# A transformer layer on one core: a second place for the turned attention output, a tile of its own for its squares, and the last group's squares from PSUM

## The chip, the core and the metric

The kernel runs on one core of one Trainium2 chip. Its engines run at the same time, each through its own queue of instructions: TensorE (PE, with its weight loads as PEld), VectorE (DVE), ScalarE (ACT), GpSimd (POOL) and SyncE (SP), which here only issues DMAs. SBUF is the on-chip memory of 128 partitions, PSUM the matmuls' accumulator memory. The metric is the device time of one execution in microseconds. Before the change it is 2869.16 us, the median of three runs (2869.08 to 2871.89).

## The reference

One layer is computed for two streams that share weights: 256 prompt tokens and 2048 latent tokens of 1024 channels. All data is float32.

```python
q, k, v, f = project(rms_norm(x, norm1_g) * (1 + sc1) + sh1, w_in, q_g, k_g)   # 4 heads, 2 halves of 64
# one head, 128 queries; latent queries see 512 cached + 2048 latent keys
s = einsum('bqhmd,bkhmd->bhmqk', q, k) / 8
p = softmax(s)                                   # for m = 0 and m = 1
a = p[:, :, 0] - lam * p[:, :, 1]
o = einsum('bhqk,bkhe->bqhe', a, v)
# the other half of the channels: real part of a 2-D DFT over positions and 128 channels
four = fft2(f, axes=(positions, channels), norm='ortho').real @ w_four
mix = concat([rms_norm(o, subln_g) * (1 - lam_init), four]) @ w_out
x = x + g1 * mix
x = x + g2 * square(relu((rms_norm(x, norm2_g) * (1 + sc2) + sh2) @ w1)) @ w2
```

The change lies in `rms_norm(o)`: for each query and head it needs the sum of the squares of the 128 outputs. Outputs are the new x of both streams and the prompt's keys and values.

## The kernel before, in words

**Stages.** The program runs the input projection (to about 470 us of the span), the DFT with its linear map (to about 517), attention (517 to about 1257), the output projection, and the MLP to the end. Float32 products are built from three matmuls of split operands (lines 94 to 97: high by high, low by high, high by low), so each operand is split beforehand into a rounded part and a rest: `ah` and `al` in attention, `woh` and `wol` for w_out, `mh` and `ml` for the mixed tokens.

**The DFT's end.** Its result stands in four tiles `ys0` to `ys3` (line 747), one for each channel group, 8192 bytes a partition each. When a tile is complete, GpSimd issues its store to the DRAM tensor `four` (line 830). These stores go through the software DMA queues, whose completion counters are called DMASW0 to DMASW7.

**Attention.** There are four heads of eight groups of 256 latent tokens, and one prompt group in each head. A latent group has two query tiles j, each with two halves m, so four stages, each with five score tiles of 128 x 512 (2560 keys). A stage runs so: PE fills five PSUM banks `Ss` (line 1081), VectorE takes the maximum of each (line 1086) and of the five (line 1089), ScalarE writes the five exponentials (line 1105) into a tile `P0` (m = 0; 10240 bytes) or two tiles `P1` (m = 1) and adds them up in `sms`. GpSimd combines P0 and P1 to the attention weights (lines 1120 and 1121). PE transposes these (line 1136), ScalarE and VectorE split the transposes into `ahs` and `als` (lines 1143 and 1148), and PE multiplies them with the values into the left half of a PSUM bank `po`.

**The end of a group**, around which the change is made: `o1` copies the output, which stands channel by token, to SBUF on ScalarE (`oTs`, line 1173). `o2` turns it on PE into the right half of the same bank (line 1177). `o3` copies the turned output to SBUF on VectorE (tile `o`, line 1181), `o4` squares its two halves on ScalarE with a sum over each row into `oss` (line 1187), and GpSimd goes on from there (`o5` to `o9`: the inverse root, a pass through DRAM that spreads it over partitions, the product with oT, and the store to the DRAM tensor `att`).

**What sets the order.** In attention every piece of work is an event with a time that is written in the code, `add(t, fn)`, in units of a stage T of 5.2. The events are sorted by that time and emitted, so the order on each engine is that of the table. For the last group (head 3, group 7, `self.last`) `o3` stands close behind `o2`, and `o4` to `o9` are kept in a list `LASTO` and called in the output projection, where the w_out splits (`w_split`, line 1560), the split of the mixed tokens (`mix`, line 1588) and the matmuls (`out_mm`, line 1599) are written one after another:

```python
mix(s0); w_split(1, 1, 4); out_mm(s0, 1, 0, 2)
for fn in LASTO[:2]: fn()          # o4, o5
w_split(1, 4); out_mm(s0, 1, 2, 4)
for fn in LASTO[2:]: fn()          # o6 to o9
```

**Where tiles lie.** Pools take SBUF one behind the other. The pool `at` (line 995) holds o, oss and the other small tiles of attention; the pool `ap` (line 996), which lies right behind it, holds the five places of P0. The DFT's pools have been given back by then, so attention's tiles lie on bytes that the DFT used, and the first user of such bytes waits until their last user is done. In the built program ys3 lies on bytes 75776 to 83967 of each partition. The first place of P0 begins at byte 83072, 896 bytes before the end of ys3.

Of the kernel before, what the change touches and what calls it, by code (L numbers as in the profile page):

```python
# [11 lines left out]
F32 = mybir.dt.float32  # L12
F32R = mybir.dt.float32r
AF = mybir.ActivationFunctionType
# [5 lines left out]
P = 128  # L20
# [21 lines left out]
def body(tc, a, out):  # L42
    nc = tc.nc
    ctx = ExitStack()
    with ctx:
# [944 lines left out]
        with ExitStack() as c3_:  # L990
# [49 lines left out]
            class Group:  # L1040
# [136 lines left out]
                        nc.tensor.transpose(self.po[:, 256 + j * P:256 + j * P + P], self.oT[:, j * P:j * P + P], ident)  # L1177

                def o3(self):
                    self.o = self.op.tile([P, 256], F32, tag="o", name=f"o{self.nm}", bufs=1)  # L1180
                    nc.vector.tensor_copy(self.o, self.po[:, 256:512])

                def o4(self):
                    self.oss = self.op.tile([P, 4], F32, tag="oss", name=f"oss{self.nm}")
                    for j in range(2):
                        o = self.o[:, j * P:j * P + P]
                        nc.scalar.activation(o, o, AF.Square, accum_out=self.oss[:, j:j + 1])

                def o5(self):
                    nc.gpsimd.tensor_add(self.oss[:, 0:2], self.oss[:, 0:2], self.s0e)  # L1190
# [115 lines left out]
            for h in range(H):  # L1306
# [19 lines left out]
                for g in range(hd.ng):  # L1326
                    gr = Group(hd, g)
                    add(base - (4 if h or g > 1 else 3) * T + 0.6 * u if base else -3.03 * T, gr.qload)
                    for st in range(4):
                        j, m = divmod(st, 2)  # L1330
# [640 lines left out]
        with ExitStack() as c6:  # L1971
# [62 lines left out]
            with tc.manual_schedule():  # L2034
                pend, NM, loaded, KS = None, 7 * 24, 4, []
                for i in range(7):
                    for b in range(3):
                        ps = [pp.tile([P, 512], F32, tag="ps", name=f"ps{i}_{b}_{j}", bufs=6) for j in range(3)]
                        for k in range(16):
# [19 lines left out]
                            if (i, b) == (6, 2) and 9 <= k < 12:  # L2059

                                j = k - 9
# [86 lines left out]
```

## Time and profile before

| | us |
|---|---|
| median of three runs | 2869.16 (2869.08 to 2871.89) |
| the profiled execution's own time | 2869.73 |
| its span in the trace | 2867.9 |
| PE busy | 2824.6 (98%) |
| VectorE busy | 1989.6 (69%) |
| ScalarE busy | 1533.1 (53%) |
| GpSimd busy | 1075.7 (38%) |
| mean granted clock of PE | 0.995 |

The profile is one execution. A row of its groups gives line, engine, operation, output and input, the count, the busy time, the mean of one in ns, and then the idle time of that engine just before these instructions with what ended most of it. A timeline row gives the start in us from the span's start, the length, the engine and the instruction, and in brackets the idle time before it with its releaser; "x4" is a run of four alike. The granted clock is a share of PE's full speed.

### The profile page before, as it was taken

To read this page: it belongs to the slowest core of one execution; us is meant where nothing else is said; L and a number is where in the kernel's file an instruction comes from. 1 tells how busy PE (TensorE), PEld (TensorE's weight loads), DVE (VectorE), ACT (ScalarE), POOL (GpSimd) and SP (SyncE) were. 2 spreads that over 40 slices of the span, in tenths; PEclk is the share of its full clock that TensorE was granted. 3 is DMA by queue.
4 is the path that set the end of the run, shared out by engine and by line. 5 is a ranking of instruction groups with operands and counts; after the bars stand their busy time and mean duration, and the time that the engine had idled before them with its cause. 6 is when DMAs were issued, how large, how long until landed. Compare 5 with 4: busy or idle time off the path is not lost.

```text
span 2867.9 us, 43210 instructions
## 1 busy us (share of the span) xinstructions
PE 2824.6 (98%) x15029; PEld 2455.1 (86%) x15029; DVE 1989.6 (69%) x3357; ACT 1533.1 (53%) x3479; POOL 1075.7 (38%) x890
## 2 busy tenths in 40 slices
PE   8999999799999999999999999999999999999999
PEld 5888888588888888888889999999998888888887
DVE  7767786688888888864477777778775354345554
ACT  4333332698998989853356565556554332233221
POOL 1211223589999899942223333333332000000000
PEclk9999999899999999999999999999999999999999
DMA  7777767331332322247777676667657464445663
GB/s 284 220 207 205 233 202 251 148 107 38 83 86 54 111 44 66 79 110 212 242 223 233 221 249 228 216 224 236 231 175 250 145 203 138 140 143 182 206 207 110
DMA packets 404492, 497.70 MB, mean 174 GB/s; under 512 B 31427, under 2 KB 320304, under 8 KB 401202
## 3 DMA queue, kind: packets, MB, share of 16 engines
q1 hardware_dynamic: 398656, 484.09, 53.5%
q0 software_dynamic: 2064, 7.67, 0.8%
q10 hardware_dynamic: 3554, 3.17, 0.3%
q8 instruction: 119, 1.95, 0.3%
q14 instruction: 99, 0.81, 0.1%
HBM read 317.30 MB, written 179.62 MB: 173 GB/s over the span
## 4 chain that ended last, share of the span: by engine, by line
PE 53%; DVE 1%; DMA 0%; issue 0%; ACT 0%; SPq 0%; POOL 0%; DVEq 0%
PE ps L95 8%; PE ps L96 8%; PE ps L97 8%; PE pB L1765 2%; PE pB L1763 2%; PE pB L1764 2%; PE pA L1763 2%; PE pC L1763 2%; PE pC L1765 2%; PE pA L1764 2%; PE pC L1764 2%; PE pA L1765 2%; PE po L97 2%; PE po L96 2%; PE po L95 2%; PE pD L1765 1%
## 5 line engine op out<-in xcount | busy, mean ns | idle before, releaser
L1086 DVE TENSOR_REDUCE mxs<-Ss 128x1 f32<-128x512 f32 x636 | 405.6, 686 | 95.3 <-PE Ss L1081 85.0
L1440 DVE TENSOR_TENSOR sl<-sr,sh 128x768 fp32r<-128x768 f32 x168 | 161.8, 964 | 331.5 <-ACT sh L1439 331.1
L1121 POOL TENSOR_TENSOR P0s<-P0s,P1s 128x1024 f32<-128x1024 f32 (+2 forms) x128 | 378.7, 2959 | 10.7
L1439 ACT CAST sh<-sr 128x768 fp32r<-128x768 f32 x168 | 140.6, 838 | 418.2 <-PE ps L96 418.2
L1805 POOL TENSOR_TENSOR gs<-g,g 128x384 f32<-128x384 f32 x48 | 69.7, 1452 | 469.4 <-ACT g L1775 389.5
L1105 ACT ACTIVATE P1s<-Ss,mxs 128x512 f32<-128x512 f32 x318 | 215.1, 693 | 40.2 <-DVE mxs L1089 38.4
L95 PE MATMUL pj<-wh,hh 128*128 128x512 f32 x576 | 228.9, 397 | 2.0 <-DVE hh L556 2.0
L95 PE MATMUL ps<-thT,sh 128*128 128x512 f32 x585 | 227.6, 389 | 0.0
L96 PE MATMUL ps<-tlT,sh 128*128 128x512 f32 x585 | 227.6, 389 | 0.0
L97 PE MATMUL ps<-thT,sl 128*128 128x512 f32 x585 | 227.6, 389 | 0.0
L96 PE MATMUL pj<-wl,hh 128*128 128x512 f32 x576 | 227.0, 394 | 0.0
L97 PE MATMUL pj<-wh,hl 128*128 128x512 f32 x576 | 225.8, 392 | 0.0
L1105 ACT ACTIVATE P0s<-Ss,mxs 128x512 f32<-128x512 f32 x318 | 214.3, 691 | 17.3 <-DMA four<-ys 16.7
L1081 PE MATMUL Ss<-KS1s,Qs 128*128 128x512 f32 x636 | 188.3, 420 | 14.8 <-ACT P0s L1105 14.5
L1136 PE MATMUL pts<-ident,P0s 128*128 128x128 f32 x1280 | 191.8, 273 | 4.8 <-DVE als L1148 1.8
L1081 PE MATMUL Ss<-KS0s,Qs 128*128 128x512 f32 x636 | 190.2, 420 | 0.4 <-ACT P1s L1105 0.4
L1774 ACT ACTIVATE g<-uz 128x384 f32<-128x384 f32 x144 | 75.8, 526 | 200.1 <-DVE uz L1797 173.7
L1136 PEld LDWEIGHTS pts<-ident,P0s 128*128 128x128 f32 x1280 | 151.4, 140 | 36.2 <-issue 4.5
L1120 POOL TENSOR_SCALAR P1s<-P1s,tots 128x1024 f32<-128x1024 f32 (+2 forms) x128 | 171.3, 1338 | 5.8
L1148 DVE TENSOR_TENSOR als<-pts,ahs 128x512 fp32r<-128x512 f32 x256 | 163.7, 681 | 8.7 <-ACT ahs L1143 8.6
L95 PE MATMUL ps<-ophT,sh 128*128 128x512 f32 x423 | 164.7, 389 | 1.1 <-DVE uz L1797 1.1
L96 PE MATMUL ps<-oplT,sh 128*128 128x512 f32 x423 | 164.6, 389 | 0.0
(535 smaller groups left out, 8020.4 us busy)
## 6 DMA issues: line engine op xcount, KB each, us to landing
sr<-sd SPq DMA_DIRECT2D x84, 768.0 KB, 4.5
a<-in_w SPq DMA_DIRECT2D x184, 256.0 KB, 4.1
sd<-gs SPq DMA_DIRECT2D x192, 192.0 KB, 1.9
sd<-g SPq DMA_DIRECT2D x144, 192.0 KB, 2.1
wm<-in_w_mod SPq DMA_DIRECT2D x32, 512.0 KB, 5.2
Qs<-qd SPq DMA_DIRECT2D x32, 512.0 KB, 5.4
b<-in_w SPq DMA_DIRECT2D x64, 256.0 KB, 5.4
b<-tsum SPq DMA_DIRECT2D x64, 256.0 KB, 4.7
```

The costliest lines, as they stand in the source:

```text
L95: nc.tensor.matmul(ps, lh, rh, start=first, stop=False)
L96: nc.tensor.matmul(ps, lh, rl, start=False, stop=False)
L97: nc.tensor.matmul(ps, ll, rh, start=False, stop=last)
L1081: nc.tensor.matmul(S[:, :w], self.Q[:, x, m, j * P:j * P + P], self.hd.KS[m][:, b * 512:b * 512 + w], start=(x == 0), stop=(x == 1))
L1086: nc.vector.tensor_reduce(self.mx[j][:, m, b:b + 1], self.S[j, m, b], axis=AX.X, op=ALU.max)
L1105: nc.scalar.activation(dst, S, AF.Exp, bias=self.mx[j][:, m, 6:7], accum_out=self.sm[j][:, m, b:b + 1])
L1120: nc.gpsimd.tensor_scalar(p, p, tot[:, 3:4], 0.0, op0=ALU.mult, op1=ALU.add)
L1121: nc.gpsimd.tensor_add(d, d, p)
L1136: nc.tensor.transpose(pt[:, c:c + P], self.p0[j][:, (kb + t) * P:(kb + t + 1) * P], ident)
L1763: nc.tensor.matmul(ps, wh[:, c], hh[:, k, :], start=first and k == 0, stop=False, skip_group_check=True)
L1764: nc.tensor.matmul(ps, wh[:, c], hl[:, k, :], start=False, stop=False, skip_group_check=True)
L1765: nc.tensor.matmul(ps, wl[:, c], hh[:, k, :], start=False, stop=k == 3, skip_group_check=True)
```

## The change

`o3` copies into one of two places for o, where there was one. For the last group it copies nothing: `o4` then reads the turned output from the PSUM bank. `o4` writes the squares, which nothing reads, into a tile `osq` of its own with one place, where before they were written over o. From there on the line numbers of the changed kernel are 3 higher.

```diff
 def o3(self):
-    self.o = self.op.tile([P, 256], F32, tag="o", name=f"o{self.nm}", bufs=1)
+    if self.last:
+        self.o = self.po[:, 256:512]
+        return
+    self.o = self.op.tile([P, 256], F32, tag="o", name=f"o{self.nm}", bufs=2)
     nc.vector.tensor_copy(self.o, self.po[:, 256:512])

 def o4(self):
     self.oss = self.op.tile([P, 4], F32, tag="oss", name=f"oss{self.nm}")
+    osq = self.op.tile([P, P], F32, tag="osq", name=f"osq{self.nm}", bufs=1)
     for j in range(2):
-        o = self.o[:, j * P:j * P + P]
-        nc.scalar.activation(o, o, AF.Square, accum_out=self.oss[:, j:j + 1])
+        nc.scalar.activation(osq, self.o[:, j * P:j * P + P], AF.Square, accum_out=self.oss[:, j:j + 1])
```

The pool `at` grows by 1024 + 512 bytes a partition, so P0's first place begins at byte 84608 in the changed program, 640 bytes behind the end of ys3.

The rows below are instructions in the order in which an engine runs them, with output, input and shape. A name ends in the tile's number in its own build, which differs between the two. Behind "waits" stand the counters that the instruction waits for before it starts: PE_49, DVE_49, Activation_49 and Pool_49 are those of the engines (an engine that waits for its own counter waits for its own earlier work), DMASW and DMAHW those of software and hardware DMA queues.

ScalarE, where the DFT ends and attention begins; L760 and L811 are copies of the DFT's last pieces. Before:

```order
L811 COPY abl_1_5204<-pabl_1_5201 128x130 [waits PE_49,Activation_49]
L760 COPY yu<-py 128x129 [waits PE_49] x2
L1105 ACTIVATE P0s_0_0_5289,sms_0_0_5266<-Ss_0_0_0_0_5268,mxs_0_0_5265 128x512 [waits DMASW0_49,DVE_49,Pool_49]
...
L1105 ACTIVATE P1s_0_0_0_5323,sms_0_0_5266<-Ss_0_0_1_0_5292,mxs_0_0_5265 128x512 [waits DVE_49,Activation_49]
...
L1105 ACTIVATE P0s_0_1_5357,sms_0_1_5330<-Ss_0_1_0_0_5332,mxs_0_1_5329 128x512 [waits DMASW7_49,DMASW3_49,DVE_49]
```

Now:

```order
L811 COPY abl_1_5204<-pabl_1_5201 128x130 [waits PE_49,Activation_49]
L760 COPY yu<-py 128x129 [waits PE_49] x2
L1105 ACTIVATE P0s_0_0_5289,sms_0_0_5266<-Ss_0_0_0_0_5268,mxs_0_0_5265 128x512 [waits DVE_49,Pool_49]
...
L1105 ACTIVATE P1s_0_0_0_5323,sms_0_0_5266<-Ss_0_0_1_0_5292,mxs_0_0_5265 128x512 [waits DVE_49,Activation_49]
...
L1105 ACTIVATE P0s_0_1_5357,sms_0_1_5330<-Ss_0_1_0_0_5332,mxs_0_1_5329 128x512 [waits DMASW4_49,DMASW3_49,DMASW7_49,DMASW0_49,DVE_49]
```

The first exponential has lost its wait on DMASW0, which stood at the count 80, that of the store of ys3. The second P0 tile now lists four such counters, DMASW0 at 64 and the others at 48. The stores' own DMAs were issued behind waits for these same counts. The second P1 tile of that place waits for DMASW5 at 64, the store of ys0, before and now.

ScalarE, at the end of one of the 31 other groups (head 0, group 1), with the copy that VectorE makes for it in the first row. Before:

```order
L1181 COPY os_1_6209<-po 128x256 [waits PE_49]
L1143 CAST ahs_2_12_6258<-pts_2_12_6242 128x512 [waits PE_49,Activation_49]
L1187 ACTIVATE os_1_6209,osss_1_6275<-os_1_6209 128x128 [waits DVE_49]
L1187 ACTIVATE os_1_6209,osss_1_6275<-os_1_6209 128x128
L1105 ACTIVATE P1s_4_0_0_6281,sms_4_0_6138<-Ss_4_0_1_0_6220,mxs_4_0_6137 128x512 [waits DVE_49,Pool_49]
...
L1143 COPY ahs_2_14_6322<-pts_2_14_6288 128x512 [waits PE_49,Activation_49]
```

Now:

```order
L1184 COPY os_1_6210<-po 128x256 [waits PE_49]
L1143 CAST ahs_2_12_6259<-pts_2_12_6243 128x512 [waits PE_49,Activation_49]
L1190 ACTIVATE osqs_1_6277,osss_1_6276<-os_1_6210 128x128 [waits DVE_49]
L1190 ACTIVATE osqs_1_6277,osss_1_6276<-os_1_6210 128x128 [waits Activation_49]
L1105 ACTIVATE P1s_4_0_0_6283,sms_4_0_6139<-Ss_4_0_1_0_6221,mxs_4_0_6138 128x512 [waits DVE_49,Pool_49]
...
L1143 COPY ahs_2_14_6324<-pts_2_14_6290 128x512 [waits PE_49]
```

The order is the old one. The second square now waits for ScalarE's own first one, and splits of transposes that come after the squares have lost such a wait.

VectorE, where attention ends and the output projection begins. Before:

```order
L1148 TENSOR_TENSOR als_7_18_14838<-pts_7_18_14816,ahs_7_18_14834 128x512 [waits DVE_49,Activation_49]
L1181 COPY os_7_14860<-po 128x256 [waits PE_49,Activation_49]
L1566 SCALAR_TENSOR_TENSOR wol_0_14923<-wout_13409,cols,woh_0_14915 128x512 [waits DMAHW6_49,Pool_49]
L1592 CAST mh_14944<-wout_13411 128x1024 [waits DMAHW2_49,DMAHW3_49,DMASW4_49,DMAHW6_49,DMASW3_49,DMAHW7_49,DMASW2_49,DMASW1_49]
L1593 TENSOR_TENSOR ml_14945<-wout_13411,mh_14944 128x1024 [waits DMAHW3_49,DVE_49]
```

Now:

```order
L1148 TENSOR_TENSOR als_7_18_14869<-pts_7_18_14847,ahs_7_18_14865 128x512 [waits DVE_49,Activation_49]
L1569 SCALAR_TENSOR_TENSOR wol_0_14952<-wout_13434,cols,woh_0_14944 128x512 [waits DMAHW6_49,Activation_49,Pool_49]
L1595 CAST mh_14973<-wout_13436 128x1024 [waits DMAHW2_49,DMAHW3_49,DMASW4_49,DMAHW6_49,DMASW3_49,DMAHW7_49,DMASW2_49,DMASW1_49]
L1596 TENSOR_TENSOR ml_14974<-wout_13436,mh_14973 128x1024 [waits DMAHW3_49,DVE_49]
L1569 SCALAR_TENSOR_TENSOR wol_1_14953<-wout_13434,cols,woh_1_14945 128x512 [waits Activation_49]
```

The copy that waited for PE's transposes is gone from VectorE's queue, and the splits behind it stand directly after the last `als`; wol_0 itself now names ScalarE, whose woh_0 it reads. On ScalarE the first of the last group's squares, in its old place behind woh_0 to woh_3 and the copy `oTs`, waits for PE where it waited for VectorE. On GpSimd the last group's sum `o5` stands one place earlier, ahead of the issue of an `att` store.

## The prediction

> **What bounds the kernel now.** I read the page first: shares by engine, then the groups with idle time before them.
>
> ```profile
> span 2867.9 us, 43210 instructions
> PE 2824.6 (98%) x15029; PEld 2455.1 (86%) x15029; DVE 1989.6 (69%) x3357; ACT 1533.1 (53%) x3479; POOL 1075.7 (38%) x890
> ...
> L1105 ACT ACTIVATE P0s<-Ss,mxs 128x512 f32<-128x512 f32 x318 | 214.3, 691 | 17.3 <-DMA four<-ys 16.7
> L1081 PE MATMUL Ss<-KS1s,Qs 128*128 128x512 f32 x636 | 188.3, 420 | 14.8 <-ACT P0s L1105 14.5
> ```
>
> PE is busy for 98%, so only a microsecond in which PE stands still or runs slowly can be won. One such hole stands out: PE waited 14.5 us for exponentials, and these had waited 16.7 us for a DMA that has nothing to do with attention, the store of the Fourier result. The timeline places it, PE, ScalarE, VectorE and GpSimd in turn:
>
> ```profile
> 520.34 0.61 PE L1081 MATMUL po<-KS1s,Qs 128*128 128x512 f32 x2
> 534.71 2.08 PE L1081 MATMUL Ss<-KS1s,Qs 128*128 128x512 f32 x4 [13.75 <-ACT P0s L1105]
> ```
>
> ```profile
> 533.88 0.69 ACT L1105 ACTIVATE P0s<-Ss,mxs 128x512 f32<-128x512 f32 x1 [16.69 <-DMA four<-ys]
> ...
> 537.80 0.69 ACT L1105 ACTIVATE P1s<-Ss,mxs 128x512 f32<-128x512 f32 x1 [0.47 <-DVE mxs L1089]
> ...
> 541.75 0.69 ACT L1105 ACTIVATE P0s<-Ss,mxs 128x512 f32<-128x512 f32 x1 [0.50 <-DVE mxs L1089]
> ...
> 545.19 0.69 ACT L1105 ACTIVATE P1s<-po,mxs 128x512 f32<-128x512 f32 x1
> ...
> 548.51 0.71 ACT L1105 ACTIVATE P0s<-Ss,mxs 128x512 f32<-128x512 f32 x1
> ```
>
> ```profile
> 520.98 0.16 DVE L1089 TENSOR_REDUCE mxs<-mxs 128x1 f32<-128x5 f32 x1
> ```
>
> ```profile
> 515.03 0.56 POOL L830 DMA_DIRECT2D four<-ys  x1 [5.56 <-DVE ys L769]
> ...
> 518.57 0.53 POOL L830 DMA_DIRECT2D four<-ys  x1 [0.34 <-issue]
> ```
>
> The landing of the first and of the last of the four stores (views of these two alone):
>
> ```profile
> DMA to landing us min/median/max: 9.7/9.7/9.7
> ```
>
> ```profile
> DMA to landing us min/median/max: 15.2/15.2/15.2
> ```
>
> The last store lands at 518.57 + 15.2 = 533.8, and the first exponential starts at 533.88. Its row maximum was there at 521.14. Then the clock, in windows (time, length, busy PE, PEld, DVE, ACT, POOL, clock, DMA):
>
> ```profile
> 523.00:524.00 1.00, 0.00 (x0) 0.00 (x0) 0.00 (x0) 0.00 (x0) 0.00 (x0) 0.53 1.01 419
> ...
> 534.00:538.00 4.00, 3.29 (x8) 2.57 (x9) 1.83 (x4) 3.53 (x11) 0.00 (x0) 0.50 0.00 1
> 540.00:545.00 5.00, 4.50 (x17) 2.53 (x15) 4.73 (x12) 4.50 (x14) 2.54 (x4) 0.99 0.03 3
> 550.00:560.00 10.00, 7.95 (x31) 4.28 (x30) 8.20 (x17) 9.66 (x28) 9.65 (x7) 1.00 0.00 1
> 600.00:1240.00 640.00, 637.00 (x4119) 541.71 (x4119) 551.76 (x1089) 574.09 (x1614) 592.70 (x473) 1.00 0.30 75
> ```
>
> Half clock until about 540, then full. From 600 to 1240 PE idles 3 us in 640 while ScalarE has 66 us free. The second hole is at attention's end, PE and then VectorE and ScalarE:
>
> ```profile
> 1254.19 0.28 PE L97 MATMUL po<-ahs,Vs 128*128 128x256 f32 x1
> 1254.94 0.44 PE L1177 MATMUL po<-ident,oTs 128*128 128x128 f32 x2 [0.46 <-ACT oTs L1173]
> 1257.32 0.77 PE L95 MATMUL po<-woh,mh 128*128 128x512 f32 x1 [1.94 <-DVE mh L1592]
> ...
> 1263.77 0.40 PE L97 MATMUL po<-woh,ml 128*128 128x512 f32 x1
> ...
> 1266.09 0.39 PE L95 MATMUL po<-woh,mh 128*128 128x512 f32 x1
> ```
>
> ```profile
> 1251.09 1.29 DVE L1148 TENSOR_TENSOR als<-pts,ahs 128x512 fp32r<-128x512 f32 x2 [2.37 <-ACT ahs L1143]
> 1255.48 0.42 DVE L1181 COPY os<-po 128x256 f32<-128x256 f32 x1 [3.10 <-PE po L1177]
> 1255.82 0.74 DVE L1566 SCALAR_TENSOR_TENSOR wol<-wout,cols,woh 128x512 fp32r<-128x512 f32 x1
> 1256.48 0.69 DVE L1592 CAST mh<-wout 128x1024 fp32r<-128x1024 f32 x1
> ...
> 1262.74 0.69 DVE L1592 CAST mh<-mT 128x1024 fp32r<-128x1024 f32 x1
> 1263.53 1.23 DVE L1593 TENSOR_TENSOR ml<-mT,mh 128x1024 fp32r<-128x1024 f32 x1
> ```
>
> ```profile
> 1251.42 2.58 ACT L1565 ACTIVATE woh<-wout,cols 128x512 fp32r<-128x512 f32 x4
> ```
>
> VectorE stood 3.10 us before the copy of the last group's turned output, with the output projection's first operands queued behind it; PE stood 1.94 us for one of these, and its clock was halved again:
>
> ```profile
> 1256.00:1257.00 1.00, 0.00 (x0) 0.00 (x0) 1.00 (x2) 1.00 (x5) 0.00 (x0) 0.96 1.01 287
> 1257.00:1263.00 6.00, 5.68 (x13) 4.01 (x14) 5.97 (x10) 6.00 (x12) 0.55 (x1) 0.50 0.94 259
> ```
>
> **The change, part by part.** *Two places for o.* The copy waits for PE alone at nearly every group (order rows above), so a second place removes no wait: 0 by itself.
>
> *What the added bytes do.* o's second place and the squares' own tile add 1024 + 512 bytes in the pool ahead of P0, so P0 slides 1536 bytes, off ys3. The order rows show it: the first exponential no longer waits on DMASW0. It then waits for its row maximum: 521.14, say 521.2. Gain 533.88 - 521.2 = 12.7 us. What is late next? The second P0 tile now lists four DMA counters, but at counts that the four stores' own issues had already waited for, so these passed by 518.57. The P1 tile that lies on ys0 needs ys0's store: 515.03 + 9.7 = 524.7, while its exponential, the third of the stage at 545.19, comes near 534 in the new time. Neither holds. On SyncE three loads of the prompt's keys and values list other counters, at counts of transfers that were over before; their order is the old one, as is that of every store.
>
> On top of it comes the clock. Four stages of five exponentials took 548.51 - 533.88 = 14.63, where the tightest took 3.32 (545.19 to 548.51), so four take 13.28 when nothing is late. The slips, 1.35 in all, begin where PE ran at 0.50. Now PE would stand only from 520.95 (520.34 + 0.61) to the first exponential's end near 521.9; the clock stayed up through idle pieces of the window 550 to 560. I take 1.0 of the 1.35 (bounds 0 and 1.35). Head: 13.7 (12.7 to 14.0).
>
> *The last group's copy leaves VectorE.* Its queue goes on after als, at 1251.09 + 1.29 = 1252.4; woh_0 is done near 1252.1. So wol_0, mh and ml, which took from 1255.82 to 1258.4, are through near 1255, when the transposes end at 1255.38. PE loses the 1.94. With idle of only 0.46 the clock should not drop: 24 steps from the first to the 25th projection matmul took 1266.09 - 1257.32 = 8.77; at the pace of the last ten, (1266.09 - 1263.77) / 10 = 0.232, they take 5.57. The 25th would start at 1255.38 + 5.57 = 1260.95, 5.1 sooner. Then VectorE is next: the second tile's mh came 1262.74 - 1255.82 = 6.9 after wol_0, so 1259.3, and up to 0.7 later because wol_4 to wol_7 still wait for ScalarE, which squares first; ml is done 2.0 later, 1261.3 to 1262.0, and PE wants it at 1261.4. I take 0.4 off: 4.7. Bounds: 1.9 (only the pause goes) and 5.1. The last group's squares, now from PSUM, start after the transposes instead of after the copy, so ScalarE comes to woh_4 a little sooner; the last group's normalisation behind them feeds token tiles that come much later, 0. On GpSimd one add of that group stands a place further ahead, also 0.
>
> A rule speaks against the larger value. The Trainium skill, TensorE: Matmul & The Clock Gate, Part 1 (The HAM clock gate), puts the fall to half clock after an idle window of about 3.4 us. By it the pieces here, 0.46 and 1.94 with work between, would not have caused the dip, and only the 1.94 would come back. The trace is quicker than that: at the head PE stopped at 520.95 and the clock was 0.53 in 523 to 524, under 3.1 us later, and here it was 0.96 over 1256 to 1257 and 0.50 after, so it fell near 1256.96, 2.5 us after the last full row of matmuls ended (1254.19 + 0.28). I follow the rows, and the other case is a rival below.
>
> *Squares into their own tile.* The second square now waits for the first, since both write one tile, 31 times and once at the end. Rows of a pair, and of a pair where the second must wait:
>
> ```profile
> 592.91 0.24 ACT L1187 ACTIVATION_READ_ACCUMULATOR os<-os 128x1 f32 x1
> 593.00 0.34 ACT L1187 ACTIVATE os<-os 128x128 f32<-128x128 f32 x1
> ...
> 593.85 0.69 ACT L1105 ACTIVATE P1s<-Ss,mxs 128x512 f32<-128x512 f32 x1 [0.42 <-DVE mxs L1089]
> ```
>
> ```profile
> 1701.05 0.53 ACT L1774 ACTIVATE g<-uz 128x384 f32<-128x384 f32 x1 [2.38 <-DVE uz L1797]
> 1701.60 0.53 ACT L1775 ACTIVATE g<-g 128x384 f32<-128x384 f32 x1
> ```
>
> In the first view the second square starts before the first one's sum is read out; in the other the second works on what the first wrote. The overlap of 0.15 (592.91 + 0.24 - 593.00) goes: 0.15 a group, 4.7 in all on ScalarE. Queued behind are the next stage's exponentials, for whose banks PE waits. Here the pair is followed by an idle 0.42, which hides it, and ScalarE has 66 us free; three or four waits for its own old work vanish too. I take 0 on PE; without that cover 4.7 lost.
>
> **Sum.** 13.7 + 4.7 = 18.4. The profiled execution took 2869.73 (span 2867.9 and 1.8 around it), 0.57 over the median of 2869.16. 2869.73 - 18.4 = 2851.3, from the median 2850.8: I say 2851.
>
> **Rivals.** *Dip stays:* the clock falls at attention's end all the same, since the short transposes and the 0.46 before them stay; 13.7 + 1.9 = 15.6, 2854. For it: between 1254.47 and 1255.38 PE still works for half the time only; against it: the clock stayed at 1.00 through 550 to 560, where PE was busy for 7.95 of 10. (The Trainium skill's rule above would end at this time too.) *Squares show:* 18.4 - 4.7 = 13.7, 2855.5. For it: ScalarE is 90% busy; against it: the idle that follows. *The wait moves:* the second P0 tile holds until the stores land, so that its stage, at 541.75 before, starts at 533.88: 7.9 + 4.7 = 12.6, 2857; were nothing freed, 4.7, 2865. For it: it lists DMASW0; against it: the counts. *Slower:* the wait between the squares costs so much that ScalarE becomes attention's bound. The 66 us that ScalarE has free are 66 / 31 = 2.1 a group; beyond these each further microsecond is PE's, and from 18.4 / 31 = 0.6 more, so from 2.7 a group, the gain is eaten up. At 3 us a group the time would be 2869.7 - 18.4 + 31 x 0.9 = 2879. For it: the wait stands 31 times in the stage that is fullest; against it: the pair at 1701, where the waiting square starts 0.02 after the first one's end (1701.05 + 0.53 to 1701.60).
>
> **How the numbers follow.** Forecast 0.68, dip stays 0.14, squares show 0.08, wait moves 0.06 (half of it at 2857), slower 0.02, other 0.02. The forecast's own range is 2849 to 2853; the rivals to 2857 belong in, and 2848 allows for more slips saved in the ramp. A measurement here tells 0.2%, 5.7 us. All cases but the slower and a remainder pass it, though 2865 does not: faster 0.95, same 0.03, slower 0.02.
>
> **What would show it.** No idle of 16 us before the first P0 exponential; it starts near 521 and PE's gap there is about 1 us at clock 1.00. The second P0 stage has no DMA as releaser. PE's 1.94 before mh is gone, and the window after it reads 1.00. Between the squares stands about 0.15. A P0 group still released by a store, or PE idle between 600 and 1240 well above 3 us, would make me wrong.

## The result, and where the time went

The changed kernel takes 2861.71 us (median of 8 runs, 2856.99 to 2863.5). The kernel before, run beside it, takes 2870.54 us (8 runs, 2867.7 to 2873.44). The ratio is 0.9967, with a 95% interval of 0.9956 to 0.9978. It is 0.3% faster, by about half of what was forecast, and outside the range of 2848 to 2857. The profiled execution took 2860.23, with a span of 2858.4 after 2867.9.

The start of attention did what was forecast. The page's groups, and the timelines of ScalarE and PE in the changed kernel:

```profile
L1105 ACT ACTIVATE P0s<-Ss,mxs 128x512 f32<-128x512 f32 x318 | 214.3, 691 | 4.9 <-DVE mxs L1089 4.0
L1081 PE MATMUL Ss<-KS1s,Qs 128*128 128x512 f32 x636 | 187.7, 420 | 1.7 <-ACT P0s L1105 1.4
```

```profile
521.25 0.69 ACT L1105 ACTIVATE P0s<-Ss,mxs 128x512 f32<-128x512 f32 x1 [4.02 <-DVE mxs L1089]
```

```profile
517.08 2.54 PE L1081 MATMUL Ss<-KS0s,Qs 128*128 128x512 f32 x10
...
522.08 1.40 PE L1081 MATMUL Ss<-KS1s,Qs 128*128 128x512 f32 x4 [1.10 <-ACT P0s L1105]
```

The DMA is gone as a releaser, the exponential starts 12.6 us sooner, and PE waits 1.10 us for it instead of 13.75.

The end of attention did it too, at first. PE there:

```profile
1240.98 0.44 PE L1177 MATMUL po<-ident,oTs 128*128 128x128 f32 x2 [0.46 <-ACT oTs L1173]
1241.17 0.48 PE L95 MATMUL po<-woh,mh 128*128 128x512 f32 x1
...
1246.86 0.39 PE L95 MATMUL po<-woh,mh 128*128 128x512 f32 x1
...
1247.84 0.50 PE L97 MATMUL po<-woh,ml 128*128 128x512 f32 x1 [0.36 <-DVE ml L1596]
```

The projection starts right behind the transposes and runs at full pace. The 25th matmul (1246.86) comes 19.2 us sooner than before. Then something happens that the prediction does not mention:

```profile
1263.62 0.39 PE L97 MATMUL po<-woh,ml 128*128 128x512 f32 x1
1271.62 1.97 PE L249 MATMUL ptb<-ident,xn 128*128 128x128 f32 x8 [7.62 <-DVE xn L236]
```

These are the transposes of the first output tile after its RMSNorm. Before the change PE stood 1.06 us at this place:

```profile
1283.63 1.09 PE L249 MATMUL ptb<-ident,xn 128*128 128x128 f32 x8 [1.06 <-DVE xn L236]
```

VectorE's scaled tile `xn` is late because GpSimd's inverse root `nrsb` (line 92) is late. GpSimd's timeline of the changed kernel shows what stands ahead of it:

```profile
1239.60 0.64 POOL L1193 TENSOR_TENSOR osss<-osss,s0es 128x2 f32<-128x2 f32 x1
1240.32 1.68 POOL L92 TENSOR_TENSOR osss<-osss,mhalf 128x2 f32<-128x2 f32 x1
1242.30 0.66 POOL L1201 DMA_DIRECT2D rs<-osss  x1 [0.29 <-POOL osss L92]
1250.33 0.55 POOL L1206 DMA_DIRECT2D rbs<-rs  x1 [7.38 <-DMA rs<-osss]
1256.56 0.73 POOL L1211 TENSOR_TENSOR oTs<-oTs,rbs 128x256 f32<-128x256 f32 x1 [5.67 <-DMA rbs<-rs]
...
1259.40 0.59 POOL L1201 DMA_DIRECT2D rs<-osss  x1 [0.29 <-POOL osss L92]
1262.77 0.54 POOL L1206 DMA_DIRECT2D rbs<-rs  x1 [2.78 <-DMA rs<-osss]
1268.57 0.72 POOL L1211 TENSOR_TENSOR oTs<-oTs,rbs 128x256 f32<-128x256 f32 x1 [5.26 <-DMA rbs<-rs]
1269.59 0.58 POOL L1215 DMA_DIRECT2D att<-oTs  x1 [0.30 <-POOL oTs L1211]
1270.20 0.58 POOL L92 TENSOR_TENSOR nrsb<-nssb,mhalf 128x1 f32<-128x1 f32 x1
```

and, on VectorE, what the root waits for:

```profile
1262.95 0.15 DVE L230 TENSOR_SCALAR nssb<-nssb 128x1 f32<-128x1 f32 x1 [1.22 <-ACT nsqb L229]
1270.81 0.75 DVE L236 TENSOR_SCALAR xn<-xo,nrsb 128x1024 f32<-128x1024 f32 x1 [7.71 <-POOL nrsb L92]
```

The mean square was there at 1263.10. The root came at 1270.20, because the last two groups' roots go through DRAM one after the other, and GpSimd waits with its whole queue for the store and then for the load, before the product and its store, twice. Before the change the same chain read:

```profile
1252.79 0.20 POOL L1190 TENSOR_TENSOR osss<-osss,s0es 128x2 f32<-128x2 f32 x1
1253.07 0.69 POOL L92 TENSOR_TENSOR osss<-osss,mhalf 128x2 f32<-128x2 f32 x1
1254.06 0.66 POOL L1198 DMA_DIRECT2D rs<-osss  x1 [0.29 <-POOL osss L92]
1259.45 0.55 POOL L1203 DMA_DIRECT2D rbs<-rs  x1 [4.73 <-DMA rs<-osss]
...
1277.79 0.58 POOL L1212 DMA_DIRECT2D att<-oTs  x1 [0.30 <-POOL oTs L1208]
1282.21 0.58 POOL L92 TENSOR_TENSOR nrsb<-nssb,mhalf 128x1 f32<-128x1 f32 x1 [3.84 <-DVE nssb L230]
```

There GpSimd was through at 1278.37 and stood 3.84 us for the mean square. Counted from the last transposes (1254.94 and 1240.98), PE's side now wants the root 5.0 us sooner (1282.11 - 1254.94 = 27.17, now 1263.10 - 1240.98 = 22.12). GpSimd is free for it 5.8 us later (1278.37 - 1254.94 = 23.43, now 1270.17 - 1240.98 = 29.19). 5.0 + 5.8 less the slack of 3.7 (1282.11 - 1278.37) makes the 7.1 us for which the root is late.

The pause also halves the clock. Windows of the changed kernel (time, length, busy PE, PEld, DVE, ACT, POOL, clock, DMA):

```profile
1240.00:1254.00 14.00, 13.18 (x60) 10.29 (x59) 13.80 (x21) 7.71 (x17) 3.13 (x4) 1.00 0.89 240
...
1271.60:1274.00 2.40, 2.38 (x10) 2.28 (x11) 1.26 (x2) 1.02 (x2) 0.00 (x0) 0.50 0.55 195
1274.00:1276.00 2.00, 2.00 (x7) 1.52 (x6) 1.18 (x3) 2.00 (x8) 0.55 (x1) 0.50 0.91 284
...
1277.00:1278.00 1.00, 1.00 (x6) 0.81 (x5) 0.59 (x1) 0.00 (x0) 0.00 (x0) 1.00 0.80 240
```

So the dip at attention's end is gone (1.00 over 1240 to 1254), and one of the same kind stands 30 us later.

The span falls into three parts by three rows of PE's timeline: attention's first matmul, the last transposes, and the first output tile's transposes. For the profiled executions:

| us | attention | transposes to first output tile | from there to the end |
|---|---|---|---|
| before | 737.90 | 28.69 | 1584.27 |
| changed | 723.90 | 30.64 | 1586.78 |
| difference | -14.00 | +1.95 | +2.51 |
| forecast | -13.7 | -4.7 | 0 |

The sum of the differences is -9.54, and attention starts 0.04 later: the 9.5 between the spans.

### The profile page after: what moved, and what is told of

Its sections match the earlier page's. It is cut to its first block, busy times and chain, and to the rows that moved or that the text cites. A ratio compares the mean times of both kernels' runs of the same rounds, so it can differ in the third digit from the quotient of the medians.

```text
span 2858.4 us, 43061 instructions
## 1 busy us (share of the span) xinstructions
PE 2822.7 (99%) x15029; PEld 2452.7 (86%) x15029; DVE 1988.8 (70%) x3356; ACT 1536.9 (54%) x3479; POOL 1077.5 (38%) x890
## 3 DMA queue, kind: packets, MB, share of 16 engines
q8 instruction: 119, 1.95, 0.3%
## 4 chain that ended last, share of the span: by engine, by line
PE 91%; DMA 4%; DVE 2%; ACT 1%; issue 1%; POOL 1%; SPq 0%; ACTq 0%; DVEq 0%; POOLq 0%
PE Ss L1081 10%; PE ps L95 8%; PE ps L97 8%; PE ps L96 8%; PE pts L1136 5%; PE po L95 4%; PE po L96 4%; PE pj L97 4%; PE po L97 4%; PE pj L96 4%; PE pj L95 4%; PE pB L1768 2%; PE pB L1767 2%; PE pB L1766 2%; PE pA L1767 2%; PE pA L1768 2%
```

## The experiments

The theory: the late root on GpSimd costs the 6.7 + 2.5 us that the last two columns lack. The rivals: the chain is late whenever attention ends early; the loads or the clock hold PE there for a reason of their own; the squares' wait for each other costs the time in attention. In the tables below the same three parts are given for each run's profile (attention starts between 516.6 and 519.3 us in them, by the stages ahead of it, so the parts compare better than the spans), and the ratio is that of its runs to runs of the kernel before on the same chip.

### Each part of the change alone

The address alone, in the kernel before:

```diff
+shift(c3_.enter_context(tc.tile_pool(name="a_pad", bufs=1)), 1024, "p")   # 1024 unused bytes
 ap = c3_.enter_context(tc.tile_pool(name="a_p", bufs=5, reuse_waits="tile"))
```

> The kernel before with 1024 unused bytes ahead of the P0 pool and nothing else: P0's first place begins at byte 84096, behind ys3. Theory (GpSimd's queue: in the changed kernel the first output tile's normalisation waits on GpSimd behind the last group's pass through DRAM, and the 7.62 us for which PE then stands, with the half clock after it, give back 9 of the 18.4): here attention and the GpSimd work behind it move together, so the first exponential starts near 521.2, PE's idle before the first output tile's transposes stays near 1.1, and the whole gain of 14.0 reaches the end: span about 2854, faster than the changed kernel. Rival (an earlier end of attention by itself makes GpSimd or the loads late): PE stands several us before those transposes here too, and the gain is 9 or less.

The last group's squares alone, in the kernel before:

```diff
 def o3(self):
     self.o = self.op.tile([P, 256], F32, tag="o", name=f"o{self.nm}", bufs=1)
+    if self.last:
+        return
     nc.vector.tensor_copy(self.o, self.po[:, 256:512])
 ...
-        nc.scalar.activation(o, o, AF.Square, accum_out=self.oss[:, j:j + 1])
+        src = self.po[:, 256 + j * P:256 + j * P + P] if self.last else o
+        nc.scalar.activation(o, src, AF.Square, accum_out=self.oss[:, j:j + 1])
```

> The kernel before with the last group's squares read from PSUM (written to o as before, one place, no own tile), P0 where it was. Theory (GpSimd's queue): the projection starts 4.6 to 5.3 us earlier in relation to attention's end, but GpSimd's chain does not come earlier, so PE stands 2 to 7.6 us before the first output tile's transposes, where it stood 1.06; the time is between 0 and 4.5 us longer than before (4.5 is what is left if the changed kernel's 9.5 is the padding's 14.0 and this part). Rival (the missing 9 us lie in attention, in the squares' wait for each other): this part alone gives its 4.7 us, span about 2863.

The changed kernel with one place for o, so that P0 lies 384 bytes inside ys3 again:

```diff
-    self.o = self.op.tile([P, 256], F32, tag="o", name=f"o{self.nm}", bufs=2)
+    self.o = self.op.tile([P, 256], F32, tag="o", name=f"o{self.nm}", bufs=1)
```

> The changed kernel with one place for o: P0's first place begins at byte 83584, 384 bytes inside ys3. Theory (the gain at attention's start is the address alone): the first exponential waits for the last store again and starts near 533.9, and the time is that of the run with the PSUM squares alone, within 1 us, since the squares' wait for each other costs PE nothing. Rival (the second place for o, or the squares' own tile, gives the gain): it starts near 521 and the time stays near the changed kernel's. Rival (the squares' wait costs): up to 4.7 us longer than the run with the PSUM squares alone.

And the changed kernel again:

> The changed kernel once more, to stand beside the other runs on the same chip. Theory: PE's idle before the first output tile's transposes is again about 7.6 us and the small store's round trip about 8 us, since both follow from the order and the loads: the time is 9 us under the kernel before. Rival (that profile caught a late DMA by chance): the idle is 1 to 3 us and the time 16 us under it.

| | median us (runs) | ratio, 95% | attention | to first output tile | to the end |
|---|---|---|---|---|---|
| address alone | 2859.07 (5) | 0.9959, 0.9946 to 0.9973 | 724.62 | 28.64 | 1584.31 |
| PSUM squares alone | 2876.09 (11) | 1.0017, 1.0009 to 1.0026 | 737.67 | 31.39 | 1586.80 |
| one place for o | 2876.20 (11) | 1.0017, 1.0008 to 1.0026 | 737.69 | 30.56 | 1585.82 |
| changed, again | 2862.75 (5) | 0.9967, 0.9955 to 0.9980 | 725.42 | 30.63 | 1585.83 |

1024 bytes that nothing reads bring at least as much as the whole change: 12.6 us by the medians and 13.3 by the parts, where 14.0 were expected. By the parts it is more than the change, which loses time in the last two; by the runs that is not clear. These five (2858.19 to 2860.33) lie below the five of the changed kernel in the same table (2861.22 to 2863.70), which ran on another chip, but among the eight of the result (2856.99 to 2863.5). Attention gets its 13.3 us there and the second part stays as long as before, so an earlier end of attention does not by itself make PE wait. It does use up GpSimd's slack: in this run GpSimd is through 27.2 us after the last transposes (1270.84 - 1243.65), where it was 23.4 before, 2.4 of that by one product that took 3.38 us instead of 0.95. The root follows with no idle before it, 0.44 behind the mean square instead of 0.10. The last group's squares from PSUM, which were to bring 4.7 us, cost 4.4 (2876.09 against 2871.66 for the kernel before): there is the loss. PE's rows at the end, of the run with the address alone and of that with the PSUM squares alone:

```profile
1246.03 0.76 PE L95 MATMUL po<-woh,mh 128*128 128x512 f32 x1 [1.94 <-DVE mh L1593]
1272.29 1.09 PE L249 MATMUL ptb<-ident,xn 128*128 128x128 f32 x8 [1.02 <-DVE xn L236]
```

```profile
1257.01 0.44 PE L1177 MATMUL po<-ident,oTs 128*128 128x128 f32 x2 [0.46 <-ACT oTs L1173]
...
1288.40 1.97 PE L249 MATMUL ptb<-ident,xn 128*128 128x128 f32 x8 [8.31 <-DVE xn L236]
```

The first keeps the pause of 1.94, and its root comes just in time; the second has lost the 1.94 and stands 8.31 before the output tile. With one place for o the first exponential waits for the store again:

```profile
533.21 0.69 ACT L1105 ACTIVATE P0s<-Ss,mxs 128x512 f32<-128x512 f32 x1 [16.34 <-DMA four<-ys]
```

So it is the address, and 384 bytes of overlap do the same as 896. This run differs from the one with the PSUM squares alone by the squares' own tile, with its wait in every group, and its median is the same to 0.1 us, its attention to 0.02. That wait costs nothing that shows. The changed kernel's second set of runs repeats the first: 7.62 us again before the output tile.

### The root ahead of the last group's product

The changed kernel, with the last group's product and store placed behind the norms of the first two output tiles. The pool that holds the last group's tiles is closed after them:

```diff
-for fn in LASTO[2:]:
+for fn in LASTO[2:4]:              # o6, o7: issue the store and the load
     fn()
 ...
-kv_even.close()                    # and the two pools that take its place
 ...
 x_norm(s1)
+for fn in LASTO[4:]:               # o8, o9: product, store
+    fn()
+kv_even.close()
 finish(s0)
```

> The changed kernel with the last group's product with its spread roots, and the store behind it, placed behind the normalisation of the first two output tiles (the pool of these tiles is closed so much later). Theory (GpSimd's queue): the root of the first output tile no longer stands behind the last group's DMA, PE's idle before the transposes falls from 7.62 to about 1, the clock stays up, and the forecast's 18.4 arrive: span about 2849.5. Rival (loads that come late, or the half clock, hold PE there for a reason of their own): the idle stays above 5 us and the span near 2858.

The same with one place for o and a squares' tile of two halves, so that no square waits for another:

> The run with the normalisation first, but with one place for o and a squares' tile of two halves, so that no square waits for another (in all groups but the last) and P0 lies at byte 84096, still behind ys3. Theory (neither the second place nor the wait between the squares is worth anything): within 1.5 us of the run with the normalisation first. Rival (the squares' wait costs PE something): up to 4.7 us less. Rival (the second place frees the copy): more time.

| | median us (5 runs) | ratio, 95% | attention | to first output tile | to the end |
|---|---|---|---|---|---|
| norm first | 2854.18 | 0.9948, 0.9935 to 0.9960 | 724.79 | 23.67 | 1584.26 |
| and squares apart | 2855.02 | 0.9942, 0.9930 to 0.9955 | 724.42 | 23.74 | 1584.27 |

GpSimd's and PE's rows of the run with the norm first:

```profile
1265.03 0.54 POOL L1206 DMA_DIRECT2D rbs<-rs  x1 [2.86 <-DMA rs<-osss]
1266.23 0.57 POOL L92 TENSOR_TENSOR nrsb<-nssb,mhalf 128x1 f32<-128x1 f32 x1 [0.66 <-DVE nssb L230]
...
1271.37 0.99 POOL L1211 TENSOR_TENSOR oTs<-oTs,rbs 128x256 f32<-128x256 f32 x1 [0.40 <-DMA rbs<-rs]
```

```profile
1267.64 1.09 PE L249 MATMUL ptb<-ident,xn 128*128 128x128 f32 x8 [0.66 <-DVE xn L236]
```

One product moved behind two roots on GpSimd gives 28.69 - 23.67 = 5.0 us in the second part, where 4.7 were forecast, and no lost clock in the third. The loads are where they were, so they were not what held PE. Two of the five runs of the norm first took 2858.79 and 2859.89, and one of the run with the squares apart 2859.22. No profile caught such a run, and what they waited for is open. The room is small in both, though: the wait for the last group's small store still stands ahead of the root in GpSimd's queue, and GpSimd was idle for only 0.66 and 0.39 us before the root in the two profiles. The medians of the two agree within 0.9 us: neither the second place for o nor the squares' wait is worth anything that shows.

### Why the chain came later

The chain is not only wanted sooner, it runs later. A view of the small store `rs` of the group before the last, issued by GpSimd, gives its time to landing before the change and after:

```profile
DMA to landing us min/median/max: 5.1/5.1/5.1
```

```profile
DMA to landing us min/median/max: 7.7/7.7/7.7
```

Before, it went out 0.9 us ahead of the last transposes, 0.8 behind the first of SyncE's loads for the projection. Now it goes out 1.3 us after the transposes and 2.3 behind that load (issued at 1253.24 and 1240.04). The run that moves it ahead of the loads leaves the norms where the change has them:

```diff
 # head 3, the group before the last two: its product and store
+if hd.h == H - 1 and g == NS // 256 - 3 and fn in (gr.o8, gr.o9):
+    t = 32.0 if fn == gr.o8 else 32.2      # were 23.4 and 26.0
```

> The changed kernel with one thing moved on GpSimd: the product of the third group from the end, which waits for a DMA, stands behind the sum, the root and the issue of the small store of the group after it, instead of ahead of them (its own store on SyncE follows two loads). The normalisation of the first output tile stays where it is in the changed kernel. Theory (GpSimd's chain of two passes through DRAM sets the late root, and it came late because that small store was issued 1.3 us after the last transposes, behind the loads): the store goes out 3 to 5 us sooner, ahead of the loads; its round trip falls from 8.0 us to about 5; the last group's product comes 6 to 8 us sooner, and PE's 7.62 us before the first output tile fall to between 0.6 and 2: span 2849.5 to 2852. Rival (the passes take their time wherever they start, and the root waits for VectorE's or SyncE's work): the idle stays above 5 us and the span near 2858.

and both moves together:

> Both moves on GpSimd in the changed kernel: the normalisation of the first two output tiles ahead of the last group's product, and the small store of the group before it issued sooner. Theory: either one already takes the wait away, so the two together give no more than one of them, within 1.5 us of each: span 2849 to 2852. Rival (each takes away a part of its own): faster than both by 2 us or more.

| | median us (5 runs) | ratio, 95% | attention | to first output tile | to the end |
|---|---|---|---|---|---|
| store sooner | 2852.86 | 0.9935, 0.9922 to 0.9947 | 724.75 | 23.63 | 1584.30 |
| both | 2852.29 | 0.9931, 0.9917 to 0.9944 | 724.63 | 23.59 | 1584.35 |

GpSimd in the run with the store sooner, and the landing of that store:

```profile
1236.73 0.20 POOL L1193 TENSOR_TENSOR osss<-osss,s0es 128x2 f32<-128x2 f32 x1 [3.45 <-ACT osqs L1190]
1237.00 0.69 POOL L92 TENSOR_TENSOR osss<-osss,mhalf 128x2 f32<-128x2 f32 x1
1237.99 0.66 POOL L1201 DMA_DIRECT2D rs<-osss  x1 [0.29 <-POOL osss L92]
...
1262.41 0.74 POOL L1211 TENSOR_TENSOR oTs<-oTs,rbs 128x256 f32<-128x256 f32 x1 [3.14 <-DMA rbs<-rs]
1263.45 0.59 POOL L1215 DMA_DIRECT2D att<-oTs  x1 [0.30 <-POOL oTs L1211]
1265.17 0.58 POOL L92 TENSOR_TENSOR nrsb<-nssb,mhalf 128x1 f32<-128x1 f32 x1 [1.14 <-DVE nssb L230]
```

```profile
DMA to landing us min/median/max: 4.8/4.8/4.8
```

and PE there:

```profile
1266.60 1.09 PE L249 MATMUL ptb<-ident,xn 128*128 128x128 f32 x8 [0.61 <-DVE xn L236]
```

The store goes out 5.0 us ahead of the last transposes of this run (1242.97) and lands in 4.8 us. The whole chain is done at 1264.04, and the root waits for PE's side again, not PE for the root. The two moves together give no more than this one (0.6 us by the medians, where 2 or more would have meant a part of its own for each): they take away one and the same wait. What they add is room: GpSimd was idle for 6.06 us before the root with both, for 1.14 with the store sooner, and none of these ten runs is as slow as the three above (2850.7 to 2853.94). That fits a root that is now and then late in those, but does not show it. Both are faster than the kernel before, by 19 us, and than the changed kernel, by 10.

Back to the change itself. There the store left 2.2 us later against the transposes than before: 0.8 because the product ahead ended so much later, 1.4 because the sum and the root behind that took 0.64 and 1.68 instead of 0.20 and 0.69. In the kernel before, VectorE stood idle from 1252.38 to 1255.48 while GpSimd ran the sum and the root; in the changed kernel VectorE works through that stretch, with this cast and a subtraction of 1.22 us behind it:

```profile
1238.95 1.25 DVE L1595 CAST mh<-wout 128x1024 fp32r<-128x1024 f32 x1
```

The cast itself takes 1.25 there, against 0.69 before the change. The Trainium skill, SBUF — State Buffer, section "SBUF: two separate sides", has a rule for this: VectorE (in some modes, or with two operands from SBUF) and GpSimd share a pair of ports as an exclusive lock, and the one that comes second stands still. The rows on both engines agree with it: the long sum ends at 1240.24, the cast at 1240.20. But no run here takes the overlap away alone, so how much of the 2.6 us that the store's landing lost comes from it, and how much from its later place among the loads, is open.

These 2.2 and 2.6 us are not all. Up to the last group's load 1.1 of them are made up, and that load adds 2.0: from its issue to the product it takes 5.80 us, where it took 3.76. In the changed kernel it goes out 0.6 us behind the first of the next token tile's loads on SyncE (1262.77 and 1262.14), before the change 8.1 us ahead of it (1272.99 and 1281.10), and it lands after 5.7 us instead of 3.6. In the runs with the store sooner and with both moves, where it is ahead of those loads again, it lands after 3.5. So 2.2 + 2.6 - 1.1 + 2.0 make the 5.8 us (the parts are rounded).

## Why the prediction was wrong, point by point

- **Head, 13.7 (12.7 to 14.0).** Right. Attention is shorter by 14.0 in the profile of the changed kernel, 12.5 in its second (just under the range), 13.3 with the address alone. The exponential came at 521.25, forecast 521.2, and neither the second P0 tile nor P1 held. 12.63 of the 14.0 us is the earlier start. Of the slips at half clock 0.9 came back, where 1.0 was taken: the first four stages took 13.72 instead of 14.63. What is left of that at attention's end varies: from the first exponential to the last transposes these runs took 719.7 to 721.2 where it was 721.06.
- **Two places for o, 0.** Right: the run with one place and the squares apart gives the same time within 0.9 us.
- **The squares' wait for each other, 0 on PE.** Right. The squares of a pair now start 0.48 apart, where it was 0.30, so the second comes 0.18 later (forecast 0.15), and an idle 0.28 follows it, where it was 0.42:

```profile
601.10 0.35 ACT L1190 ACTIVATE osqs<-os 128x128 f32<-128x128 f32 x1
601.31 0.23 ACT L1190 ACTIVATION_READ_ACCUMULATOR osqs<-os 128x1 f32 x1
601.58 0.31 ACT L1190 ACTIVATE osqs<-os 128x128 f32<-128x128 f32 x1
...
602.26 0.69 ACT L1105 ACTIVATE P1s<-Ss,mxs 128x512 f32<-128x512 f32 x1 [0.28 <-DVE mxs L1089]
```

- **The copy leaves VectorE, 4.7, with the dip gone.** Right as far as the step looked. PE loses the 1.94, the clock stays at 1.00 through an idle piece of 0.46, the 25th matmul comes 5.3 sooner against the transposes, and PE waits 0.36 for `ml`, where 0.4 was taken off. With nothing behind it late, the part is worth 5.0.
- **The step that failed** is the sentence on the last group's squares: "the last group's normalisation behind them feeds token tiles that come much later, 0". It asked who reads the result, and that is indeed late. It did not ask what is queued behind the normalisation on GpSimd: the roots of the output tiles' norms, in order, behind two passes through DRAM. GpSimd's slack there was 3.84 us, visible in the trace of before as the idle time in front of `nrsb`. Moving PE 4.7 us ahead of the chain spends that even if the chain keeps its time, and the chain lost 5.8 us as well. The true price of this part in the changed kernel is +1.95 and +2.5 of clock instead of -4.7.
- **The rivals.** "Dip stays" was wrong about the dip; "squares show" and "the wait moves" named the wrong places. The rival on the slower side put a limit on ScalarE; the part that did lose time was on GpSimd, which the prediction had ruled out in one clause.

## What to carry to other kernels

When a stage is made to start sooner, list what each in-order queue still has to do before the next stage's first need, and compare its slack with the gain: here 4.7 us were to be won against a slack of 3.8 on GpSimd. The slack is not a fixed sum either: with the address alone it was gone as well, with no change in the order. A wait for a DMA on an engine's queue is a wait for everything behind it, so here the small pass through DRAM belonged ahead of the bulk loads, and its consumer behind the urgent work. A wait on a transfer that has nothing to do with the work can be an address: 1024 spare bytes gave at least as much here as the whole change.

## What the runs showed that was not expected

- The 1 KB store took 4.7 and 4.8 us to land when it was issued ahead of the loads (both moves, store sooner), 5.1 and 5.4 at 0.8 us behind the first load (the kernel before, the address alone), and 7.2 to 8.4 at 2.3 behind (the six other profiles, 7.7 in that of the changed kernel).
- Two small operations of GpSimd took two to three times as long beside a working VectorE: 0.64 against 0.20 and 1.68 against 0.69. In the run with the address alone one product of 128 x 256 took 3.38 us, where it took 0.73 in the changed kernel and 0.95 before, while VectorE split the rows of w_out from 1253.39 to 1258.54:

```profile
1255.76 3.38 POOL L1209 TENSOR_TENSOR oTs<-oTs,rbs 128x256 f32<-128x256 f32 x1 [6.41 <-DMA rbs<-rs]
```

- The half clock after the pause of 7.62 us held PE's work from 1271.6 to about 1277 and cost 2.5 us (the last column of the tables); in the changed kernel's second profile it held from 1274.0 to about 1277 and cost 1.6. The one after the 1.94 us at attention's end cost 3.1: 24 steps of the projection took 8.77, and 1246.86 - 1241.17 = 5.69 without it.
- The clock fell sooner than the prediction's bound for the head. Before the change it was 1.00 over 522 to 523 and 0.53 over 523 to 524. If it knows only full and half there, it fell near 523.06, an estimate from these two figures: 2.1 us after PE stopped at 520.95.
